# Embedding gate: bias added on VectorE, gate block by block, projection behind the third FFN group, and a norm that subtracts over both halves first

## The chip, the cores and the metric

The kernel runs on one core of one Trainium2 chip. The metric is device time in microseconds (us) from the start to the end of one execution, as a median over runs. In the text PE is TensorE (matmuls), PEld its weight loads, DVE is VectorE, ACT is ScalarE, POOL is GpSimd and SP is SyncE, which issues the DMAs.

## The reference, cut to what matters

A decoder of two layers works on x of 256 tokens by 1024 features in float32. Each layer is FFN, mixer, FFN and an embedding step, each followed by a norm. The mixer is forgetting attention in layer 0 and latent attention (MLA) in layer 1; neither is changed.

```python
def post_norm(x, delta, g, b):
    return layer_norm(ALPHA * x + delta, g, b)

for i in range(DEPTH):
    ...
    x = post_norm(x, 0.5 * swiglu(x, ffn1_w_in[i], ffn1_w_out[i]), ln_g[i, 0], ln_b[i, 0])
    ...                                     # the mixer, with its norm ln_g[i, 1]
    x = post_norm(x, 0.5 * swiglu(x, ffn2_w_in[i], ffn2_w_out[i]), ln_g[i, 2], ln_b[i, 2])
    gate = jax.nn.sigmoid(x @ ple_w_gate[i] + ple_b_gate[i])
    x = post_norm(x, gate * (p[i] @ ple_w_proj[i]), ln_g[i, 3], ln_b[i, 3])
```

`ple_w_gate` is 1024 x 1024 per layer, `ple_b_gate` one row of 1024, `p[i]` 256 x 256 and `ple_w_proj` 256 x 1024. A `layer_norm` needs mean and variance over the 1024 features of a token, then (x - mean) * rstd * g + b.

## The kernel before

**Tiles.** The 256 tokens are two tiles, t = 0 and 1, of 128 partitions; `x[t]` is 128 x 1024. `xT` holds x transposed, which matmuls use as the stationary operand (`L473` is the transpose on PE, `XT(t)` does one tile in two halves of four). Each product is formed in three matmuls (`mm3`, `L469`): every operand is split into a high part in a short-mantissa form (ACT copies, `L163` for weights, `L478` for activations) and a low part (DVE subtracts, `L164` and `L479`), and high x high, high x low and low x high are added in PSUM.

**Weights.** `Stream` loads weights in groups into three staging buffers (`raw`, DMAs on SP) in the order in which they are first used. It splits a unit into one of ten slots (`hl`), or into larger tiles that are lent to it while nobody else uses them (`ota`, `otb`, `qk`, `fs`). A slot comes free after the last use of its unit. `pump`, called after each `mm3`, emits the next split when a slot is free, its load has arrived by the planner's clock, and the planned time of ACT and DVE is at most 1.6 us ahead of PE's; `use` forces a split that is still missing. So the order of splits among other work on ACT and DVE is set as the program is written out, by planned times that `S.busy` keeps. `tl` gets a tile by its tag; a tag with one buffer (`PT`, `gb`) waits for the last reader of what it held.

**PSUM.** `bank` hands out eight banks: four `y`, two `h`, two `tr`.

**FFN** (`ffn`): 11 chunks of 256 features. `H` and `HT` compute a chunk's gate and up projections, `W` adds its part of the output. Chunks 0 and 1 come first, then groups (2, 3, 4), (5, 6, 7), (8, 9, 10), each followed by the `W` of finished chunks; `W` of chunks 8 to 10 runs for tile 0, then its norm is emitted, then for tile 1, with `XT(0)` inside. `at` lists work to do ahead of a chunk. `EDGE` gives the number of dummy transposes of the identity ahead of the first chunk of the second and third group.

**Embedding step.** `ple_load` (ahead of chunk 4 of the second FFN) loads p, `ple_transpose` (chunk 5) transposes it, `ple_project` (chunk 8) multiplies it with `ple_w_proj` in `h` banks, four results of 128 x 512, which ACT copies to `pj` (`L736`). `ple` then does the gate for tile 0 ("row 0") and tile 1 ("row 1"). It first puts the bias into the banks: the bias row is a weight unit of one partition (`pb`), and a row of ones as stationary operand spreads it over 128 partitions, in two matmuls per block (high and low part). The gate matmuls follow, for each k of 8 over both blocks of 512 columns; in layer 1, row 1 goes block by block in four quarters of 256. `post` takes the sigmoid (`L764`), multiplies by the projection (`L765`), adds to x (`L530`) and takes statistics (`L531`). `ln_apply` merges them (`L539`, `L540`), takes the power on POOL (`L541`) and applies the norm in four DVE passes over halves (`L546`): subtract mean and multiply by g, then multiply by rstd and add b. It does half 0 entirely, then half 1, except in the kernel's last norm (`last`), where both subtractions come first. `load_gb` loads g and b, spread over the partitions, once the tile `gb` is free. Behind layer 0's embedding step stands layer 1's first FFN, which begins with the key/value projection (`kv_down`).

Of the kernel before, what the change touches and what calls it, by code (L numbers as in the profile page):

```python
# [15 lines left out]
D = 1024  # L16
# [236 lines left out]

WIDTH = {"kd": 1280, "dq": 1536, "kq": 1280, "kvv": 1024, "ff": 1024, "pb": 64}

# [12 lines left out]
def unit_of(key, raw):  # L268

    k, u = key[0], key[-1] % 2  # L270
    if k in ("win", "fv"):
        return raw.rearrange("p (k c) -> p k c", c=512)[:, 2 * u : 2 * u + 2, :], 128, 1024
    if k in ("wout", "fo", "pg", "pp", "mo", "qr"):
        return raw[:, 1024 * u : 1024 * u + 1024], 128, 1024
    if k in ("fk", "fq"):
        return raw.rearrange("p (k c) -> p k c", c=256)[:, :, 128 * u : 128 * u + 128], 128, 1024
    if k == "pb":
        return raw[0:1, 0:1024], 1, 1024
# [12 lines left out]
    raise KeyError(key)  # L291


def make_loads(a):
# [3 lines left out]
    def loads(q, g, raw, fine, between):  # L298
# [25 lines left out]
        elif k in ("wout", "fo", "pg", "pp", "mo"):  # L324
# [10 lines left out]
            q.dma_start(raw.rearrange("p (k c) -> p k c", c=1024), rows(w, 2 * i, 2))  # L335
        elif k == "pb":
            q.dma_start(raw[0:1, 0:1024], a["ple_b_gate"][g[1] : g[1] + 1, :])
        elif k == "kd":
# [43 lines left out]
class Trunk:  # L382
# [33 lines left out]
    def setup(self):  # L416
# [5 lines left out]
        self.mhalf = one([128, 1], F32, "mhalf")  # L422
        self.ones = one([1, 128], F32R, "ones")
        self.xT = one([128, 2, 2, 8, 128], F32R, "xT")
# [15 lines left out]
        for c0 in (0, 256):  # L440
# [3 lines left out]
            )  # L444
        nc.gpsimd.memset(self.ones.bitcast(F32), 1.0)
        self.S.lend("ota", "otb", "qk", "fs")
# [86 lines left out]

    def ln_apply(self, t, st, eps, last=False):
        nc = self.nc
# [7 lines left out]
        hs = [slice(512 * n, 512 * n + 512) for n in range(2)]  # L543
        for i, n in ((0, 0), (0, 1), (1, 0), (1, 1)) if last else ((0, 0), (1, 0), (0, 1), (1, 1)):
            xs = self.x[t][:, hs[n]]
            nc.vector.scalar_tensor_tensor(  # L546
                xs, xs, rs if i else mv[:, 0:1], self.gb[:, i, hs[n]],
                op0=ALU.mult if i else ALU.subtract, op1=ALU.add if i else ALU.mult,
            )
# [8 lines left out]
    def ffn(self, li, which, lni, kv=False, at=None, cold=False):  # L558
# [125 lines left out]
        for group in GROUPS:  # L684
            for c in group:
                for f in at.get(c, ()):
                    f()
                if c == 4:
                    self.load_gb(li, lni)
                HT(c, (lambda: T(1)) if c == 2 else None, EDGE[li, which] if c == group[0] > 2 else 0)  # L690
            if kv and done == 0:
                self.flush()
                self.kv_transpose()
            while done < min(group[-1] + 1, n - STAG):
                W(done, both)
                done += 1
        for c in range(n - STAG, n):
            W(c, (0,))
# [24 lines left out]
    def ple_project(self, li):  # L723
# [14 lines left out]
    def ple(self, li, last):  # L738
        nc, S = self.nc, self.S
        y, st = {}, {}  # L740

        def bias(t, blocks):
            w = self.use(("pb", li))
            for c0, c1 in blocks:
                y[t, c0] = self.bank("y")
                for i in range(2):
                    self.mm(
                        y[t, c0][:, 0 : c1 - c0], self.ones, w[0:1, i, c0:c1], i == 0, False
                    )

        def gate(t, k, blocks):
            w = self.use(("pg", li, k))
            for c0, c1 in blocks:
                self.mm3(
                    y[t, c0][:, 0 : c1 - c0], lambda i: self.xT[:, t, i, k, :],
                    lambda i: w[:, i, c0:c1], False, k == 7,
                )

        def post(t, c0, c1):
            if t not in st:  # L760
                st[t] = [self.tl([128, 4, 6], F32, "st4", 2), self.tl([128, D], F32, "g4", 5), 0]
            s, sg, j = st[t]
            g = sg[:, c0:c1]
            nc.scalar.activation(g, y[t, c0][:, 0 : c1 - c0], AF.Sigmoid)  # L764
            nc.vector.tensor_tensor(g, g, self.pj[:, 2 * t + c0 // 512, c0 % 512 : c0 % 512 + c1 - c0], op=ALU.mult)  # L765
            self.ln_stats(s[:, j, :], t, c0, c1 - c0, g, ALPHA)
            self.S.busy(act=c1 - c0, dve=c1 - c0)
            st[t][2] = j + 1

        full = ((0, 512), (512, 1024))  # L770
        bias(0, full)
        for k in range(8):
            if k == 6:
                self.XT(1)
            gate(0, k, full)
        for c0, c1 in full:
            post(0, c0, c1)
        self.ln_apply(0, st[0][0][:, 0:2, :], LN_EPS)
        quarters = tuple((c, c + 256) for c in range(0, 1024, 256))
        bias(1, full if not last else quarters)  # L780
        if not last:
            for k in range(8):
                if k == 6:
                    self.XT(0)
                gate(1, k, full)
            for c0, c1 in full:
                post(1, c0, c1)
            self.ln_apply(1, st[1][0][:, 0:2, :], LN_EPS)
            S.lend("ota")
        else:  # L790
            self.store(0)
            for c0, c1 in quarters:
                for k in range(8):
                    gate(1, k, ((c0, c1),))
                post(1, c0, c1)
            self.ln_apply(1, st[1][0], LN_EPS, True)
            self.store(1)
# [289 lines left out]
    def kv_setup(self):  # L1087
        self.kvn = self.tl([128, QR], F32, "nrm", 1)[:, 0:256]
        if not self.rec:
            self.dma(self.kvn, pbcast(self.a["kv_norm"], 256))  # L1090
            for t in range(2):
                self.dma(self.rope[:, t], self.a["rope"][128 * t : 128 * t + 128])
        self.kvtok = self.tl([128, 2, 768], F32, "PT", 1)

    def rms_scale(self, src, n, junk):
# [279 lines left out]
    def run(self):  # L1375
# [4 lines left out]
            5: [self.ple_transpose],  # L1380
            8: [lambda: self.ple_project(li)],
        }
# [68 lines left out]
```

## Time and profile before

| | |
|---|---|
| median of 3 runs (lowest, highest) | 1101.17 us (1100.28, 1101.95) |
| span of the profiled execution | 1100.3 us; no other time is given for it |
| mean granted clock of TensorE | 0.997 |
| PE / PEld busy | 1080.1 us (98%) / 976.7 us (89%) |
| DVE / ACT / POOL busy | 711.5 us (65%) / 542.5 us (49%) / 79.7 us (7%) |
| HBM read | 196.81 MB, 180 GB/s over the span |

How to read the rows shown further on. A row of the timeline has the start in us from the start of the span, the time to the end of the last of the merged instructions, engine, source line, operation, output<-inputs, shapes and count; in brackets stands the engine's idle time ahead of it and what ended that. A row of the groups by line has count | busy us, mean ns | idle us ahead, and what ended it. Matmuls overlap, so a stream of them is read by the distance of their starts. Line numbers are those of the kernel above.

### The profile page before, as it was taken

To read this page: it belongs to the slowest core of one execution; us is meant where nothing else is said; L and a number is where in the kernel's file an instruction comes from. 1 tells how busy PE (TensorE), PEld (TensorE's weight loads), DVE (VectorE), ACT (ScalarE), POOL (GpSimd) and SP (SyncE) were. 2 spreads that over 40 slices of the span, in tenths; PEclk is the share of its full clock that TensorE was granted. 3 is DMA by queue.
4 is the path that set the end of the run, shared out by engine and by line. 5 is a ranking of instruction groups with operands and counts; after the bars stand their busy time and mean duration, and the time that the engine had idled before them with its cause. 6 is when DMAs were issued, how large, how long until landed. Compare 5 with 4: busy or idle time off the path is not lost. (4 is left out here: it accounts for less than half of the span.)

```text
span 1100.3 us, 17702 instructions
## 1 busy us (share of the span) xinstructions
PE 1080.1 (98%) x7186; PEld 976.7 (89%) x7186; DVE 711.5 (65%) x1006; ACT 542.5 (49%) x790; POOL 79.7 (7%) x130
## 2 busy tenths in 40 slices
PE   9999999999999999999999999998999999999997
PEld 6989998899879899997899999987899789898986
DVE  5765545788896555458975453487766885454576
ACT  5554433567645534434655353345655474445421
POOL 0000000313100000001320000011111000000000
PEclk9999999999999999999999999999999999999998
DMA  8896652553458756445677564353533678555502
GB/s 280 282 294 223 214 185 72 162 165 135 145 170 279 253 198 191 154 163 163 187 259 245 190 193 143 104 150 107 162 111 111 215 245 276 177 187 175 182 8 77
DMA packets 150676, 199.00 MB, mean 181 GB/s; under 512 B 11842, under 2 KB 128578, under 8 KB 150596
## 3 DMA queue, kind: packets, MB, share of 16 engines
q1 hardware_dynamic: 150596, 197.88, 55.6%
q8 instruction: 56, 0.92, 0.3%
q14 instruction: 24, 0.20, 0.1%
HBM read 196.81 MB, written 1.05 MB: 180 GB/s over the span
## 5 line engine op out<-in xcount | busy, mean ns | idle before, releaser
L164 DVE TENSOR_TENSOR hl<-raw,hl 128x1024 fp32r<-128x1024 f32 (+3 forms) x287 | 334.5, 1184 | 172.5 <-ACT hl L163 171.7
L163 ACT ACTIVATE hl<-raw 128x1024 fp32r<-128x1024 f32 (+3 forms) x287 | 286.9, 1021 | 198.6 <-PE y L469 82.2
L469 PE MATMUL h<-xT,hl 128*128 128x256 f32 x2016 | 239.9, 278 | 1.7 <-DVE P L613 0.7
L469 PEld LDWEIGHTS h<-xT,hl 128*128 128x128 f32 x2016 | 234.1, 188 | 3.7 <-DVE P L613 0.9
L469 PE MATMUL y<-hl,g 128*128 128x512 f32 x816 | 189.6, 390 | 0.0
L469 PEld LDWEIGHTS y<-hl,g 128*128 128x128 f32 x816 | 152.2, 188 | 31.0
L469 PE MATMUL tr<-xT,hl 128*128 128x256 f32 x864 | 102.0, 277 | 0.0
L469 PEld LDWEIGHTS tr<-xT,hl 128*128 128x128 f32 x864 | 100.0, 188 | 0.1
L469 PE MATMUL h<-hl,xT 128*128 128x512 f32 (+1 forms) x396 | 94.7, 388 | 0.4 <-DVE hl L164 0.3
L469 PEld LDWEIGHTS h<-hl,xT 128*128 128x128 f32 x396 | 72.1, 188 | 17.1 <-DVE hl L164 2.2
L541 POOL TENSOR_TENSOR rs<-ve,mhalf 128x1 f32<-128x1 f32 x16 | 15.2, 951 | 827.1 <-DVE ve L540 827.1
L469 PE MATMUL y<-hl,xT 128*128 128x512 f32 (+2 forms) x312 | 61.0, 351 | 0.0
L469 PEld LDWEIGHTS y<-hl,xT 128*128 128x128 f32 x312 | 50.8, 188 | 7.9 <-issue 0.7
L478 ACT ACTIVATE xT<-tr 128x512 fp32r<-128x512 f32 x36 | 20.2, 597 | 58.9 <-PE tr L473 58.9
L479 DVE TENSOR_TENSOR g<-P,g 128x512 fp32r<-128x512 f32 x36 | 24.9, 693 | 34.5 <-ACT g L478 34.5
L478 ACT ACTIVATE g<-P 128x512 fp32r<-128x512 f32 x36 | 22.8, 634 | 40.3 <-DVE P L648 29.4
L164 DVE TENSOR_TENSOR otb<-raw,otb 128x1024 fp32r<-128x1024 f32 (+1 forms) x20 | 24.1, 1203 | 18.9 <-ACT otb L163 18.9
L469 PE MATMUL y<-hl,ota 128*128 128x512 f32 x144 | 36.0, 393 | 0.0
L164 DVE TENSOR_TENSOR qk<-raw,qk 128x1024 fp32r<-128x1024 f32 x21 | 25.8, 1230 | 14.4 <-ACT qk L163 14.4
L469 PE MATMUL tr<-xT,qk 128*128 128x256 f32 x264 | 31.9, 277 | 0.0
L479 DVE TENSOR_TENSOR xT<-tr,xT 128x512 fp32r<-128x512 f32 x36 | 23.3, 683 | 13.3 <-ACT xT L478 13.3
L469 PEld LDWEIGHTS tr<-xT,qk 128*128 128x128 f32 x264 | 30.9, 188 | 0.0
(232 smaller groups left out, 1371.0 us busy)
## 6 DMA issues: line engine op xcount, KB each, us to landing
raw<-in_ffn_w_in_dram SPq DMA_DIRECT2D x172, 512.0 KB, 4.9
raw<-in_ffn_w_out_dram SPq DMA_DIRECT2D x44, 1024.0 KB, 5.1
raw<-in_fox_w_in_dram SPq DMA_DIRECT2D x12, 1024.0 KB, 5.3
raw<-in_ple_w_gate_dram SPq DMA_DIRECT2D x8, 1024.0 KB, 5.0
raw<-in_mla_w_o_dram SPq DMA_DIRECT2D x8, 1024.0 KB, 6.0
gb<-in_ln_g_dram SPq DMA_DIRECT2D x8, 512.0 KB, 6.3
gb<-in_ln_b_dram SPq DMA_DIRECT2D x8, 512.0 KB, 7.4
raw<-in_fox_w_o_dram SPq DMA_DIRECT2D x4, 1024.0 KB, 5.1
```

The lines of the kernel that those rows point to most:

```text
L163: nc.scalar.activation(hi[:, c], src[:, c], AF.Copy)
L164: nc.vector.tensor_tensor(lo[:, c], src[:, c], hi[:, c].bitcast(F32), op=ALU.subtract)
L469: self.nc.tensor.matmul(out, lhsT, rhs, start=start, stop=stop)
L478: self.nc.scalar.activation(hi, src, AF.Copy)
L479: self.nc.vector.tensor_tensor(lo, src, hi.bitcast(F32), op=ALU.subtract)
L541: nc.gpsimd.tensor_tensor(rs, ve, self.mhalf, op=ALU.pow)
```

## The change

The bias row is loaded by `ple_load` as one broadcast DMA of 512 KB into the tile `PT`, and DVE adds it to each block as it leaves PSUM; the sigmoid then works in place, from SBUF. The weight unit `pb`, the row of ones and the one-row matmuls are gone. `kv_setup` no longer takes `PT`; `kv_down(0)` does, after `ple`. The gate runs block by block in both rows: all eight k for one block, `post` for it, then the next block. Layer 1's row 1 has blocks of 512, 256 and 256. `XT(1)` stands ahead of k = 4 of row 0's second block; in layer 0, row 1's first `post` is put off until `XT(0)`, ahead of k = 3 of the second block. `ple_project` runs behind chunk 10, ahead of the last `W` products, in `tr` banks. `EDGE` is keyed by FFN and chunk: the second FFN has 1 dummy transpose at chunk 5 as before and 4 instead of 1 at chunk 8; the first has 4 at both, as before. `ln_apply` always does both subtractions first.

```diff
+FULL = ((0, 512), (512, 1024))
-EDGE = {(0, "ffn1"): 4, (0, "ffn2"): 1, (1, "ffn1"): 4, (1, "ffn2"): 1}
+EDGE = {("ffn1", 5): 4, ("ffn1", 8): 4, ("ffn2", 5): 1, ("ffn2", 8): 4}
...
-        for i, n in ((0, 0), (0, 1), (1, 0), (1, 1)) if last else ((0, 0), (1, 0), (0, 1), (1, 1)):
+        for i, n in ((0, 0), (0, 1), (1, 0), (1, 1)):
...
-                HT(c, (lambda: T(1)) if c == 2 else None, EDGE[li, which] if c == group[0] > 2 else 0)
+                HT(c, (lambda: T(1)) if c == 2 else None, EDGE.get((which, c), 0))
...
+        for f in at.get(n, ()):
+            f()
         for c in range(n - STAG, n):
             W(c, (0,))
...
+        self.bg_row = self.tl([128, 2, 768], F32, "PT", 1).rearrange("p a b -> p (a b)")[:, 0:D]
+        if not self.rec:
+            self.dma(self.bg_row, pbcast(self.a["ple_b_gate"][li], D))
...
-                ps = self.bank("h")
+                ps = self.bank("tr")
...
-        def bias(t, blocks):
-            w = self.use(("pb", li))
-            for c0, c1 in blocks:
-                y[t, c0] = self.bank("y")
-                for i in range(2):
-                    self.mm(
-                        y[t, c0][:, 0 : c1 - c0], self.ones, w[0:1, i, c0:c1], i == 0, False
-                    )
...
+                if k == 0:
+                    y[t, c0] = self.bank("y")
                 self.mm3(
                     y[t, c0][:, 0 : c1 - c0], lambda i: self.xT[:, t, i, k, :],
-                    lambda i: w[:, i, c0:c1], False, k == 7,
+                    lambda i: w[:, i, c0:c1], k == 0, k == 7,
                 )
-        def post(t, c0, c1):
+        def post(t, *blocks):
             if t not in st:
                 st[t] = [self.tl([128, 4, 6], F32, "st4", 2), self.tl([128, D], F32, "g4", 5), 0]
+            sg = st[t][1]
+            for c0, c1 in blocks:
+                g = sg[:, c0:c1]
+                nc.vector.tensor_tensor(g, y[t, c0][:, 0 : c1 - c0], self.bg_row[:, c0:c1], op=ALU.add)
+                nc.scalar.activation(g, g, AF.Sigmoid)
+            for c0, c1 in blocks:
+                scaled(t, c0, c1)
+
+        def scaled(t, c0, c1):
             s, sg, j = st[t]
             g = sg[:, c0:c1]
-            nc.scalar.activation(g, y[t, c0][:, 0 : c1 - c0], AF.Sigmoid)
             nc.vector.tensor_tensor(g, g, self.pj[...], op=ALU.mult)
             self.ln_stats(s[:, j, :], t, c0, c1 - c0, g, ALPHA)
...
+        def row(t, blocks, at={}):
+            for i, (c0, c1) in enumerate(blocks):
+                for k in range(8):
+                    if (i, k) in at:
+                        at[i, k]()
+                    gate(t, k, ((c0, c1),))
+                if (i, 8) not in at:
+                    post(t, (c0, c1))
+            self.ln_apply(t, st[t][0][:, 0 : len(blocks), :], LN_EPS)
+
+        row(0, FULL, {(1, 4): lambda: self.XT(1)})
         if not last:
+            def between():
+                self.XT(0)
+                post(1, FULL[0])
+            row(1, FULL, {(0, 8): None, (1, 3): between})
             S.lend("ota")
         else:
             self.store(0)
+            row(1, ((0, 512), (512, 768), (768, 1024)))
             self.store(1)
...
     def kv_down(self, t):
+        if t == 0:
+            self.kvtok = self.tl([128, 2, 768], F32, "PT", 1)
...
-            8: [lambda: self.ple_project(li)],
+            NCH: [lambda: self.ple_project(li)],
```

More of the change, by code (lines that the diff above doesn't have):

```diff
@@ L422, in setup @@
         self.mhalf = one([128, 1], F32, "mhalf")
-        self.ones = one([1, 128], F32R, "ones")
         self.xT = one([128, 2, 2, 8, 128], F32R, "xT")
@@ L532, in ln_stats, with ln_apply @@
         self.S.busy(dve=2 * w)
-    def ln_apply(self, t, st, eps, last=False):
+    def ln_apply(self, t, st, eps):
         nc = self.nc
@@ L740, in ple @@
         y, st = {}, {}
-        def bias(t, blocks):
-            w = self.use(("pb", li))
-            for c0, c1 in blocks:
-                y[t, c0] = self.bank("y")
-                for i in range(2):
-                    self.mm(
-                        y[t, c0][:, 0 : c1 - c0], self.ones, w[0:1, i, c0:c1], i == 0, False
-                    )
+        quarters = tuple((c, c + 256) for c in range(0, 1024, 256))
         def gate(t, k, blocks):
@@ L762, in post @@
+        def scaled(t, c0, c1):
             s, sg, j = st[t]
             g = sg[:, c0:c1]
[L764 removed]
             nc.vector.tensor_tensor(g, g, self.pj[:, 2 * t + c0 // 512, c0 % 512 : c0 % 512 + c1 - c0], op=ALU.mult)
             self.ln_stats(s[:, j, :], t, c0, c1 - c0, g, ALPHA)
[L767 removed]
+            self.S.busy(act=c1 - c0, dve=2 * (c1 - c0))
             st[t][2] = j + 1
[L770 removed]
@@ L771, in ple @@
[L771 to L780, printed above, removed]
-        if not last:
[L782 to L788, printed above, removed]
+        def row(t, blocks, at={}):
[7 more added lines that the diff above has]
+            self.ln_apply(t, st[t][0][:, 0 : len(blocks), :], LN_EPS)
@@ L791, in ple @@
             self.store(0)
[L792 to L796, printed above, removed]
+            row(1, ((0, 512), (512, 768), (768, 1024)))
             self.store(1)
```

8 lines of the change are left out of this document (1 added, 7 removed).

## The prediction

> **What bounds the kernel now.** I read the page first, then the time by stages, the groups by line, and last the timeline at the places that the diff touches.
>
> ```profile
> span 1100.3 us, 17702 instructions
> PE 1080.1 (98%) x7186; PEld 976.7 (89%) x7186; DVE 711.5 (65%) x1006; ACT 542.5 (49%) x790; POOL 79.7 (7%) x130
> ```
>
> TensorE (PE) is busy in 98% of the span, so a matmul taken out saves its time, as long as the next matmul's operands are there earlier too. That condition decides this case, and the stages show where it is weak.
>
> ```profile
> 502.00:513.80 11.80, 11.80 (x55) 9.30 (x54) 10.04 (x17) 3.52 (x7) 0.92 (x1) 1.00 0.73 235
> 513.80:528.00 14.20, 14.20 (x66) 11.23 (x65) 12.29 (x18) 7.75 (x10) 0.92 (x1) 1.00 0.43 137
> 536.00:550.00 14.00, 14.00 (x75) 12.16 (x75) 12.82 (x15) 9.42 (x15) 9.12 (x12) 1.00 0.67 212
> ```
>
> Columns: stretch, length, then busy time of PE, PEld, DVE, ACT, POOL. Over the whole span VectorE (DVE) is busy 65%; in the embedding step of layer 0 and the FFN behind it, it is busy 85 to 92% (10.04 of 11.80, 12.29 of 14.20, 12.82 of 14.00), and that is where the change gives it more work. PE is not idle there at all, at a granted clock of 1.00.
>
> **A. The bias matmuls go.** Three stretches in the timeline: projection of the FFN, bias, gate of row 0 in layer 0; and gate, bias, gate at row 1 of layer 1.
>
> ```profile
> 500.72 1.64 PE L469 MATMUL y<-hl,g 128*128 128x512 f32 x6
> 503.42 1.65 PE L469 MATMUL y<-hl,xT 128*128 128x512 f32 x6
> 1009.03 5.61 PE L469 MATMUL h<-hl,g 128*128 128x512 f32 x24
> 1076.62 3.01 PE L469 MATMUL y<-hl,xT 128*128 128x512 f32 x12
> 1080.74 11.57 PE L469 MATMUL y<-hl,xT 128*128 128x256 f32 x96
> L469 PE MATMUL y<-hl,ones 1*128 1x256 f32 (+1 forms) x12 | 2.5, 336 | 0.0
> L469 PE MATMUL y<-fs,ones 1*128 1x512 f32 x8 | 2.4, 419 | 0.0
> ```
>
> The row of 24 gives the pitch of 512-column matmuls: (5.61 - 0.39) / 23 = 0.227 us, where 0.39 is one matmul's length; the row of 96 gives (11.57 - 0.28) / 95 = 0.119 for 256 columns. Six at 0.227 from 500.72 end at 502.08 and the gate starts at 503.42: four one-row matmuls hold PE for 1.34, not for 4 x 0.227 = 0.91, so changing to and from the one-row form costs about 0.4 more. Row 1 of layer 1: 1076.62 + 12 x 0.227 = 1079.34, gate at 1080.74, 1.40. The 20 bias matmuls stand in four such groups: 3 x 1.34 + 1.40 = 5.4 us off PE. Bounds: 4.5 (pitch alone) and 5.4. Layer 1's first two quarters become one block: 24 x 0.227 = 5.45 for 48 x 0.119 = 5.71, 0.2 less. Sum -5.6. The splitting of the bias row (one ACT and one DVE pass per layer) and its turn in the three staging buffers go as well, off the path.
>
> **B. The projection moves; one edge grows.** Before, it stood ahead of chunk 8 and its evacuation held that chunk's bank.
>
> ```profile
> 1014.50 0.95 PE L469 MATMUL h<-xT,hl 128*128 128x256 f32 x6
> 1015.65 5.21 PE L469 MATMUL h<-xT,hl 128*128 128x256 f32 x42 [0.20 <-ACT ota L736]
> 1048.96 4.29 PE L469 MATMUL y<-hl,g 128*128 128x512 f32 x18
> 1050.49 1.05 ACT L163 ACTIVATE hl<-raw 128x1024 fp32r<-128x1024 f32 x1
> L736 ACT ACTIVATE ota<-h 128x512 f32<-128x512 f32 x8 | 4.8, 595 | 3.5 <-PE h L469 3.5
> 1075.83 1.04 PE L473 MATMUL tr<-ident,x 128*128 128x128 f32 x8
> ```
>
> Six matmuls from 1014.50 at 0.119 end at 1015.21; the next starts at 1015.65: 0.44 lost per layer, -0.9 for two. Chunk 8 gets three more dummy transposes: (1.04 - 0.27) / 7 = 0.11 each, 6 x 0.11 = +0.65, since I see no wait there for them to fill. The projection itself costs the same 24 matmuls, but now the third of its four results needs the bank of the first back, 12 x 0.227 = 2.72 after its start. Where it will start, the projection of chunk 8 starts today (1048.96), and ACT splits a weight until 1050.49 + 1.05 = 1051.54; behind that in ACT's queue the evacuation takes 0.60, to 1052.14, and the bank is wanted at 1051.68: 0.5 of waiting, twice, +1.0 (0 if the split comes later, 1.5 if two come first). Its weights' load and two splits move with it behind three chunks on SP, ACT and DVE; they are wanted 35 us later as well. B is +0.75, between -0.25 and +1.25.
>
> **C. Every norm subtracts over both halves first.** The last norm of the kernel has that order already, so both orders stand in the timeline.
>
> ```profile
> 1059.77 0.74 DVE L546 SCALAR_TENSOR_TENSOR x<-x,mv,gb 128x512 f32<-128x512 f32 x1
> 1060.95 0.75 DVE L546 SCALAR_TENSOR_TENSOR x<-x,rs,gb 128x512 f32<-128x512 f32 x1 [0.44 <-POOL rs L541]
> 1062.41 0.75 DVE L546 SCALAR_TENSOR_TENSOR x<-x,rs,gb 128x512 f32<-128x512 f32 x1
> 1094.51 1.40 DVE L546 SCALAR_TENSOR_TENSOR x<-x,mv,gb 128x512 f32<-128x512 f32 x2
> 1095.84 1.41 DVE L546 SCALAR_TENSOR_TENSOR x<-x,rs,gb 128x512 f32<-128x512 f32 x2
> 309.87 0.63 PE L473 MATMUL tr<-ident,x 128*128 128x128 f32 x4 [0.82 <-DVE x L546]
> 728.08 0.63 PE L473 MATMUL tr<-ident,x 128*128 128x128 f32 x4 [0.66 <-DVE x L546]
> 870.08 0.75 DVE L546 SCALAR_TENSOR_TENSOR x<-x,rs,gb 128x512 f32<-128x512 f32 x1 [1.15 <-DMA gb<-in_ln_b_dram]
> 875.22 1.19 PE L469 MATMUL h<-qk,xT 128*128 128x512 f32 x4 [0.29 <-DVE xT L479]
> 899.72 2.33 PE L469 MATMUL h<-xT,hl 128*128 128x256 f32 x18 [0.69 <-DVE P L613]
> ```
>
> Old order: 1059.77 to 1063.16, 3.39. New: 1094.51 to 1097.25, 2.74. So 15 norms get 0.65 shorter, and their first half is ready 0.14 later (2.07 against 1.93 after the start). That pays only where PE waits for a norm. At 309.87 and 728.08 it waits for the second half: 0.65 at the first; at the second I take 0.2 (estimate), because the next V product waits behind the norm in DVE's queue for work that POOL holds anyway. At 870.08 the norm waits for its late bias row; with both subtractions first, that wait is filled, and PE's waits of 0.29 and 0.69 behind it should go, 1.0 together. C is -1.9, between 0 (another late operand takes each wait's place) and -2.5.
>
> **D, E. VectorE's new work.** The nearest rows for an add out of a bank are the FFN's products, for the sigmoid the old one.
>
> ```profile
> L648 DVE TENSOR_TENSOR P<-P,h 128x512 f32<-128x512 f32 x20 | 13.8, 688 | 20.8 <-PE h L469 12.7 <-ACT P L647 8.1
> L613 DVE TENSOR_TENSOR P<-P,h 128x256 f32<-128x256 f32 x16 | 6.6, 415 | 4.7 <-ACT P L612 4.7
> L764 ACT ACTIVATE g<-y 128x512 f32<-128x512 f32 x6 | 3.5, 600 | 0.4
> L164 DVE TENSOR_TENSOR hl<-raw,hl 128x1024 fp32r<-128x1024 f32 x255 | 308.7, 1229 | 165.5 <-ACT hl L163 165.1
> 509.68 0.75 DVE L546 SCALAR_TENSOR_TENSOR x<-x,rs,gb 128x512 f32<-128x512 f32 x1
> 522.74 0.75 DVE L546 SCALAR_TENSOR_TENSOR x<-x,rs,gb 128x512 f32<-128x512 f32 x1
> 525.00 1.03 PE L473 MATMUL tr<-ident,x 128*128 128x128 f32 x8
> 503.42 0.73 ACT L163 ACTIVATE hl<-raw 128x640 fp32r<-128x640 f32 x1
> 511.08 0.82 DVE L164 TENSOR_TENSOR hl<-raw,hl 128x640 fp32r<-128x640 f32 x1
> 1086.79 0.75 DVE L546 SCALAR_TENSOR_TENSOR x<-x,rs,gb 128x512 f32<-128x512 f32 x1
> 1092.35 0.38 ACT L764 ACTIVATE g<-y 128x256 f32<-128x256 f32 x1 [2.44 <-PE y L469]
> ```
>
> A block of 512 now takes DVE 0.69 (add), about 0.7 idle for the sigmoid (0.60 and two hand-overs), and three passes of 0.69: 3.5; a block of 256 takes 0.42 + 0.5 + 1.3 = 2.2. Behind a waiting add stand the splits of coming weights and the low part of the next transposed rows.
>
> Layer 0 (D), on the old clock with the bias out: row 0 starts at 502.1, row 1 at 502.1 + 48 x 0.227 + 0.87 (eight transposes) = 513.8. DVE's norm of the FFN's second tile, 510.4 before, ends at about 510.0; block 0 then runs to 513.5, the low parts of row 1's input (two passes, 1.3) to 514.8, one queued split to 516.0. Row 1's third matmul wants the first low part at 514.3 and has it at 514.2: just in time. Block 1 to 519.5, statistics 0.4, norm 2.74: first half ready at 522.0. The transposes of tile 0 stand 33 matmuls into row 1, 521.3 (before there was room: norm done 523.49, transposes 525.00). So +0.8. The gate's weights are now kept until row 1's second block, 5.4 us longer, so three splits that DVE could do early go behind that norm. With DVE at 88%, PE 2.7 us ahead of its old time must give some of it back in the first FFN chunks: I take 1.1. D is +1.9, between 0 and 2.7, where layer 0's whole saving is lost.
>
> Layer 1 (E): row 1 ends 3 us earlier, but its three blocks come after the norm of tile 0. That starts from row 0's end, 1079.34 today less its own bias group of 1.34, 1078.0, and 0.1 more until DVE has it; it takes 3.5 + 0.4 + 2.74: 1084.7 (before 1087.54). Then 3.5 + 2.2 + 2.2: 1092.6. From the last sigmoid's end (1092.73) to the norm's end (1097.25) is 4.5 today, 1.3 of it three passes over 256; the rest, 3.2, follows as it is: 1095.8, 1.45 earlier than 1097.25. Of the 2.95 that A gives layer 1 (1.34 + 1.40 + 0.2), 1.5 is lost. E is +1.5, between 0.5 and 2.9.
>
> The broadcast of the bias row is 512 KB more on SP ahead of the norm's rows at chunk 4, some 1.6 us at the 343 GB/s of this stretch:
>
> ```profile
> 355.00:365.00 10.00, 10.00 (x91) 10.00 (x90) 6.42 (x7) 6.10 (x7) 0.00 (x0) 1.00 1.01 343
> ```
>
> I cost it at nothing: chunk 4's weights are split by then, and chunk 5 is 30 us off; with that cover gone it is 1.6 per layer. The wait of the key/value copy for the bias row's last reader is nothing: that add is done a norm earlier.
>
> **Sum.** -5.6 + 0.75 - 1.9 + 1.9 + 1.5 = -3.35. The profiled execution has no other time beside its span of 1100.3, which is 0.9 below the runs' median of 1101.17; so 1097.0 for the span and 1097.8 for the median.
>
> D and E rest on DVE taking its work in order. The rows above show it once: the split whose high part ACT ended at 504.15 got its low part at 511.08, behind the whole norm that ended at 510.43. [...]
>
> **Rivals.** (1) All hidden: DVE catches up in layer 0, the bank's wait in B does not come: D 0, B -0.25: -6.25, span 1094.05, median 1094.9. For it: DVE has 3 us free in those 28; against: its new work comes in waits, not only in busy time. (2) DVE is the clock of the whole step: D 2.7, E 2.9, C 0.4 of its 1.9: -5.6 + 0.75 - 0.4 + 5.6 = +0.35, no change: 1101.5. The norms then do not do what they say. For it: 12.82 of 14.00; against: PE never waits there today. (3) Slower: the kept slots. Row 1's first block frees no slot, and if the FFN's first four splits, 4 x 1.23 = 4.9, all land behind its last norm and on PE's path, D is 2.7 + 4.9; with E 2.9 and C as forecast: -5.6 + 0.75 - 1.9 + 7.6 + 2.9 = +3.75, 1104.9. It decides from 4 us on PE's path beyond D's 2.7; against it: a first-sweep order that asks for high parts first.
>
> **Chances.** 0.2% is 2.2 us, about what a measurement of this kernel can tell. Forecast (-2.2 to -5) 0.45, its own range 1096.2 to 1099.0; rival 1 0.2; rival 2 0.25; rival 3 0.1. So faster 0.65, same 0.25, slower 0.1. Range: rival 1 with C at its bound of -2.5, 1094.3, to rival 2, 1101.5.
>
> **What would show it.** A: no one-row matmuls, PE's gate directly behind the projection. B: a wait of the projection on ACT ota of about 0.5. C: norms of 2.74, no PE wait near 309 and 899. D: PE waiting on DVE x or xT near 520 and on hl near 540. E: DVE, not PE, ending the last chain, the last add starting over 1 us after its matmuls. The prediction is wrong if PE waits more than 3 us between 500 and 550, or if the chain ends on PE.

## The result, and the profile after

Median 1095.34 us after (1094.80 to 1095.58, 4 runs) against 1101.01 us before (4 runs): ratio 0.9947, 95% interval 0.9935 to 0.9959, 5.7 us faster. Measured a second time, the same pair gave 1094.40 against 1101.69 (`r_after`, below), ratio 0.9934 (0.9921 to 0.9946). The forecast was 1097.8, range 1094.3 to 1101.5: the time lies in the range, but below the forecast's own band of 1096.2 to 1099.0, and the gain is 2.3 us larger than the sum. Two executions of each kernel were profiled (the second ones are the runs `r_before` and `r_after`), and the second of before is what explains the difference. From the page of after:

```profile
span 1093.6 us, 17616 instructions
PE 1072.9 (98%) x7148; PEld 970.6 (89%) x7148; DVE 712.1 (65%) x1010; ACT 539.3 (49%) x787; POOL 81.3 (7%) x129
## 4 chain that ended last, share of the span: by engine, by line
DVE 1%; ACT 0%; issue 0%; DVEq 0%
```

The same line of the chain in before:

```profile
PE 17%; DVE 2%; DMA 1%; ACT 1%; issue 1%; SPq 0%; POOL 0%; DVEq 0%; ACTq 0%
```

PE lost 7.2 us of busy time between these two profiles, and 5.2 between the second ones (1077.4 to 1072.2). The chain that ended last is new in kind: as far back as it is traced (16 us) it holds no PE at all. The end of layer 1 belongs to DVE and ACT now.

To see where the time went, I cut the span at events that both kernels have, and compare the lengths of the pieces (worked out from the timelines; the times named are those of the first profile of before, and a chunk counts from the start of its silu):

| stretch | before, 1st | before, 2nd | after, 1st | after, 2nd |
|---|---|---|---|---|
| start to chunk 2 of the first FFN, 0 to 43.2 | 43.20 | 43.79 | 43.62 | 42.89 |
| to the transposes at 308.4 | 265.22 | 265.15 | 265.36 | 265.07 |
| norm there, to the transposes at 320.0 | 11.54 | 11.54 | 10.76 | 10.70 |
| to chunk 7 of the second FFN, 428.2 | 108.26 | 108.24 | 108.24 | 108.30 |
| chunks 8 to 10, projection, to the transposes at 499.9 | 71.70 | 70.43 | 70.78 | 70.82 |
| embedding step of layer 0, to chunk 2 at 570.0 | 70.05 | 70.13 | 68.07 | 68.07 |
| to the transposes at 726.8 | 156.85 | 156.85 | 156.84 | 156.84 |
| latent attention and its norms, to 910.0 | 183.21 | 182.50 | 182.00 | 181.53 |
| to chunk 7, 992.3 | 82.24 | 82.25 | 82.24 | 82.24 |
| chunks 8 to 10, projection, to 1064.0 | 71.70 | 70.43 | 70.78 | 70.79 |
| embedding step of layer 1, to PE's last matmul | 28.34 | 28.34 | 25.23 | 25.23 |
| to DVE's last pass | 4.93 | 4.93 | 6.57 | 6.58 |
| to the end of the span | 3.08 | 3.07 | 3.07 | 3.08 |
| span | 1100.32 | 1097.65 | 1093.56 | 1092.15 |

Most pieces repeat to 0.1 us; the start and the latent attention vary more. Three things stand out. The embedding step shrinks as forecast. The end on DVE grows as forecast. And chunks 8 to 10 take 71.70 us in one execution of the kernel before and 70.43 in the other, in both layers: the same program, 1.27 us apart each time. The prediction was made on the longer of the two.

**Two paces.** Rows of 96 matmuls of 256 columns: in the first profile of before (one of chunks 5 to 7, then one of 8 to 10), in the second, and in after:

```profile
406.89 11.04 PE L469 MATMUL h<-xT,hl 128*128 128x256 f32 x96
473.61 11.47 PE L469 MATMUL h<-xT,hl 128*128 128x256 f32 x96
```
```profile
473.29 11.04 PE L469 MATMUL h<-xT,hl 128*128 128x256 f32 x96
```
```profile
1026.88 11.04 PE L464 MATMUL h<-xT,hl 128*128 128x256 f32 x96
```

With 0.28 as one matmul's length the pitch, the time from start to start, is (11.47 - 0.28) / 95 = 0.1178 us in the row at 473.61 and 0.1133 in the others. In the first profile of before the granted clock is 1.00 in both its rows, from 406.89 to 417.90 us and from 473.61 to 484.90. Once it has settled, a stream here keeps its pace ("rhythm" in the expectations) to its last matmul (each row of 24 from 459 to 473 us takes 2.99 us in the first profile of before and 2.88 in the second): 288 x 0.0045 = 1.3 us for chunks 8 to 10, each layer.

### The profile page after: what moved, and what is told of

Its sections match the earlier page's. It is cut to its first block, busy times and chain, and to the rows that moved or that the text cites. A ratio compares the mean times of both kernels' runs of the same rounds, so it can differ in the third digit from the quotient of the medians.

```text
span 1093.6 us, 17616 instructions
## 1 busy us (share of the span) xinstructions
PE 1072.9 (98%) x7148; PEld 970.6 (89%) x7148; DVE 712.1 (65%) x1010; ACT 539.3 (49%) x787; POOL 81.3 (7%) x129
## 5 line engine op out<-in xcount | busy, mean ns | idle before, releaser
L464 PE MATMUL h<-xT,hl 128*128 128x256 f32 x2064 | 243.7, 278 | 1.0 <-DVE qk L474 0.6
L464 PEld LDWEIGHTS h<-xT,hl 128*128 128x128 f32 x2064 | 238.3, 188 | 2.4 <-DVE qk L474 0.8
L464 PE MATMUL y<-hl,g 128*128 128x512 f32 x804 | 186.6, 390 | 0.0
L464 PE MATMUL tr<-xT,hl 128*128 128x256 f32 x840 | 98.9, 277 | 0.0
L464 PEld LDWEIGHTS tr<-xT,hl 128*128 128x128 f32 x840 | 96.9, 188 | 0.1
L464 PE MATMUL y<-hl,xT 128*128 128x512 f32 (+2 forms) x276 | 57.8, 363 | 0.0
L464 PEld LDWEIGHTS y<-hl,xT 128*128 128x128 f32 x276 | 47.5, 188 | 7.4
L164 ACT ACTIVATE qk<-raw 128x1024 fp32r<-128x1024 f32 x21 | 22.2, 1058 | 19.3 <-PE tr L464 6.6
L464 PE MATMUL tr<-xT,otb 128*128 128x256 f32 x264 | 31.7, 276 | 0.0
L464 PEld LDWEIGHTS tr<-xT,otb 128*128 128x128 f32 x264 | 30.7, 188 | 0.0
```

Of the source, the lines that this page charges most:

```text
L164: nc.scalar.activation(hi[:, c], src[:, c], AF.Copy)
L464: self.nc.tensor.matmul(out, lhsT, rhs, start=start, stop=stop)
```

## The experiments

They ran on three chips; a ratio is to the kernel before on the same chip. Its medians there were 1099.29 (e1 to e4), 1101.69 (`r_before`, `r_after`, e7, e8) and 1099.03 us (e5, e6, e9, e10). The changed kernel itself ran beside e7 and e8 only, so what e2, e4, e6, e9 and e10 change against it is read from stretches of the trace.

**e2, one dummy transpose in the changed kernel.**

```diff
-EDGE = {..., ("ffn2", 5): 1, ("ffn2", 8): 4}
+EDGE = {..., ("ffn2", 5): 1, ("ffn2", 8): 1}
```

> The changed kernel with one dummy transpose instead of four ahead of chunk 8 of the second FFN; the projection stays behind chunk 10. Theory (rhythm set by the transposes): chunks 8 to 10 fall back to 118 ns, +1.3 us a layer, less 0.33 for the three transposes: +1.0 a layer, +2.0 us in all, ratio to the changed kernel 1.0018, to the kernel before 0.9965. Rival (the wait on ACT ota or the projection ahead of the chunk sets the rhythm): they stay at 113.7, and three transposes less give -0.33 a layer, -0.65 in all, ratio to the kernel before 0.994.

Median 1096.44, ratio 0.9974 (0.9964 to 0.9984). Its timeline:

```profile
443.74 0.27 PE L468 MATMUL h<-ident 128*128 128x128 f32 x1
443.77 11.55 PE L464 MATMUL h<-xT,hl 128*128 128x256 f32 x96
472.12 5.82 PE L464 MATMUL h<-xT,hl 128*128 128x256 f32 x48
```

(5.82 - 0.28) / 47 = 0.1179: the slower pace, in both layers, and chunks 8 to 10 with the projection take 71.72 us, 0.94 more than in the changed kernel, as the theory said (+1.0). So moving the projection does not by itself bring the quicker pace, and the slower one does not need the wait on ACT `ota` ahead of the chunk: there is none here.

**e1, four dummy transposes in the kernel before.**

```diff
-EDGE = {(0, "ffn1"): 4, (0, "ffn2"): 1, (1, "ffn1"): 4, (1, "ffn2"): 1}
+EDGE = {("ffn1", 5): 4, ("ffn1", 8): 4, ("ffn2", 5): 1, ("ffn2", 8): 4}
...
```

> The kernel before, with four dummy transposes instead of one ahead of chunk 8 of each layer's second FFN; the projection stays where it was, directly ahead of them. Theory (rhythm): the number of transposes ahead of a run of 256-column matmuls settles at which of two rhythms, 113.3 or 118 ns from start to start, it goes through. Then chunks 8 to 10 go from 118.1 to 113.7 ns a matmul, 288 x 4.6 ns = 1.3 us a layer; 3 more transposes at 0.11 take 0.33 of it, or fill part of the 0.44 wait on ACT ota. Net -1.0 to -1.3 a layer, -2.0 to -2.6 us in all, ratio 0.998. Rival (wait): the slow rhythm comes from the projection's wait on ACT ota ahead of the chunk, so the chunks stay at 118 and the time goes up by 0 to 0.65 us. Rival (no rhythm): the change's 2.6 us beyond the forecast of part B lie elsewhere; no change of the distance from chunk 8 to chunk 10.

The stretch of chunks 8 to 10 is 70.43 us in both layers, 1.27 less than in the first profile of before. The three dummies fill most of the wait on ACT `ota` (3 x 0.11 of 0.44, an estimate from the rows of before), so this run alone doesn't tell the theory from the rival; the next one does. Where they fill a wait they cost nothing: the second profile of before, with one, has the same 70.43. But the median is 1100.35, ratio 1.0012 (1.0002 to 1.0022), not the 0.998 expected. The kernel before took 1099.29 on that chip, near the 1099.43 of the execution that was profiled in the quicker pace, so there may have been nothing left to gain; no execution of it was profiled there. In e1's trace the piece of latent attention and norms takes 184.1 us, 1.6 more than in the second profile of before, and the chunks nothing; that piece varies from profile to profile, as e3 shows.

**`r_before` and `r_after`, both kernels once more.**

> The kernel before once more, for the rhythm of chunks 8 to 10 behind one dummy transpose. If one transpose leaves the rhythm open (e3 went through them at 113.7 ns with one, the kernel before and e2 at 118), it can come out either way here, and the span shows it: about 1100.3 us at 118, 1097.7 at 113.7. If the rhythm is fixed by the program, 118 again and a span of 1100.

The pace is 113 ns this time, span 1097.65, and the wait ahead of chunk 8 is there all the same:

```profile
452.09 7.76 PE L469 MATMUL h<-xT,hl 128*128 128x256 f32 x66 [0.19 <-ACT ota L736]
```

The same row of the first profile, at 451.60, takes 8.04. So the wait does not bring the slower pace, and e2 has that pace without the wait: the rival of e1 and e2 is out. The profiled run (1099.43) is one of the lowest of the kernel's runs on that chip; the other ten of `r_before` took 1101.4 to 1103.0.

> The changed kernel once more, beside the others of this call. With four transposes ahead of every group the rhythm is 113.7 ns in all six late chunks of both second FFNs: median 1093.5 to 1095.5 us, ratio to the kernel before 0.995 to 0.997 (less than the first 0.9947 if the kernel before is in the fast rhythm on this chip).

1094.40, ratio 0.9934. Runs of the changed kernel lie within 0.4 us here, those of the kernel before within 4.3.

Over all 14 profiles, eight groups of chunks each: behind four or five transposes (102 groups) the pace settles at 113 ns in every one; behind a single one (chunk 8, ten groups in five executions) it is 118 in both layers of before, e2 and e8, and 113 in both layers of `r_before` and e3. So one transpose leaves the pace open, and four settled it. What decides it stays open. It is not a property of the execution as a whole: the first 24 matmuls of chunk 2, behind four transposes of data, settle at 118 ns in some FFNs and at 113 in others of one execution (in after 118 at 32.5 us and 113 at 334.7), so the number of transposes is not all of it either.

**e5, part B alone.** The kernel before with the projection behind chunk 10 in `tr` banks, and four dummies at chunk 8.

```diff
-            8: [lambda: self.ple_project(li)],
+            NCH: [lambda: self.ple_project(li)],
```

> The kernel before with part B alone: projection behind chunk 10 on the other pair of banks, four dummy transposes ahead of chunk 8. Theory (rhythm is left open by one transpose and settled by four): chunks 8 to 10 at 113.7 ns in both layers in this and every execution; to an execution of the kernel before in the fast rhythm the part costs what the record said, +0.75 us (its two waits for a bank and six more transposes, less the stall ahead of chunk 8), to one in the slow rhythm it gains 1.9. So a profiled span of about 1098.4 (fast execution of before 1097.65 + 0.75), the ratio of medians 0.998 to 1.0007, by how many executions of before fall in the slow rhythm. Rival (part B is a gain by itself, whatever the rhythm): span under 1096.

Median 1100.81, ratio 1.0013 (1.0004 to 1.0022), 1.8 us longer and above the 0.998 to 1.0007 expected: alone, part B gains nothing. The stretch takes 70.79 us in both layers, 0.72 more in sum than in the execution of before with the quicker pace, 1.8 less than in the one with the slower. In the profiled run another 1.2 over `r_before` lies again in the stretch of latent attention. The medians of e1 and e5 are near their profiled runs, so this is no single outlier; whether the edits bring it about or the chip does is not shown.

**e3 and e4, the norms' order.** e3 is the kernel before with only the new order, e4 the changed kernel with the old one.

```diff
-        for i, n in ... if last else ((0, 0), (1, 0), (0, 1), (1, 1)):
+        for i, n in ((0, 0), (0, 1), (1, 0), (1, 1)):
```

> The kernel before, with only the norms' new order (both halves subtracted first, then both scaled): part C alone. By the traces of before and after: -0.78 at the transposes of layer 0 near 309 us, about -0.35 net near 728, -0.86 near 875 to 900; in sum -2.0 us, ratio 0.998, if the parts add up; on the record of the prediction -1.9. At the end of layer 1 the norms of 2.74 instead of 3.39 also let the second row's products start sooner, but there TensorE bounds the kernel before, so nothing more. Rival: the gain at 309, 728 and 900 came from the rows' new timing and not from the order; then 0 to -0.8.

Ratio 0.9984 (0.9975 to 0.9992), -1.8 us. Against the second profile of before, 0.79 of it is at the transposes of 309 us and 0.96 in the latent attention. At 309, the second profile of before and the first of after:

```profile
310.39 0.63 PE L473 MATMUL tr<-ident,x 128*128 128x128 f32 x4 [0.82 <-DVE x L546]
```
```profile
308.98 1.29 PE L468 MATMUL tr<-ident,x 128*128 128x128 f32 x8
```

All eight transposes now run as one group; the wait for the second half is gone. The latent attention begins with the same case. The second profile of before, and the first of after:

```profile
727.39 0.63 PE L473 MATMUL tr<-ident,x 128*128 128x128 f32 x4 [0.67 <-DVE x L546]
```
```profile
723.66 1.23 PE L468 MATMUL tr<-ident,x 128*128 128x128 f32 x8
```

From these transposes to the next group on another tile (744.86 in the first profile of before) PE takes 18.03 to 18.08 us in the six profiles with the old order and 17.39 to 17.42 in the eight with the new: 0.65, in every execution. The rest of the stretch depends on two broadcast rows, g and b of a norm near 870 us, which in some executions arrive late. In e5 (old order) the norm waits for both, in after for one:

```profile
868.26 0.75 DVE L546 SCALAR_TENSOR_TENSOR x<-x,mv,gb 128x512 f32<-128x512 f32 x1 [0.74 <-DMA gb<-in_ln_g_dram]
869.67 0.75 DVE L546 SCALAR_TENSOR_TENSOR x<-x,rs,gb 128x512 f32<-128x512 f32 x1 [0.66 <-DMA gb<-in_ln_b_dram]
```
```profile
865.12 1.42 DVE L541 SCALAR_TENSOR_TENSOR x<-x,mv,gb 128x512 f32<-128x512 f32 x2 [0.36 <-DMA gb<-in_ln_g_dram]
```

How late they are changes from profile to profile, and in `r_before` neither is waited for. The whole stretch took 182.5 to 184.1 us in the six profiles with the old order and 181.5 to 182.4 in the eight with the new (e2 is the 182.4).

> The changed kernel with the old order of the norms' passes (all but the last norm). If part C is worth 2.0 us by itself, +2.0 us and, since VectorE now bounds the last row, 0.65 more for each of the two norms that stand in its chain near the end (FFN tile 1, gate tile 0): +3.3 us at the most; 0.65 more in layer 0 if VectorE is late there too (transposes near 520 us). So +2.0 to +4 us, ratio to the changed kernel 1.002 to 1.0035. Rival (order only matters where TensorE waits, and those waits are covered otherwise in the changed kernel): under +1 us.

1100.37, ratio 1.0009 (1.0001 to 1.0018): without the new order the whole change is worth nothing on that chip. Against the two profiles of after its span, less the differing start, is 5.5 and 6.2 us longer, outside my +2 to +4. 2.9 of that is layer 0's embedding step:

```profile
521.92 0.63 PE L468 MATMUL tr<-ident,x 128*128 128x128 f32 x4 [0.17 <-DVE x L541]
523.37 0.63 PE L468 MATMUL tr<-ident,x 128*128 128x128 f32 x4 [0.82 <-DVE x L541]
542.65 0.73 PE L464 MATMUL h<-hl,xT 128*128 128x512 f32 x2 [0.70 <-DVE hl L165]
543.91 3.37 PE L464 MATMUL h<-hl,xT 128*128 128x512 f32 x20 [0.53 <-DVE hl L165]
```

DVE's chain there starts 0.4 later, behind the norm of the FFN's tile 0; three more norms stand in it, each 0.65 longer, and the splits behind them take 0.5 more: 2.9. PE waits for that chain at tile 0's transposes and in the next FFN. In the changed kernel only one such wait is left (below).

**e8, part A alone.** e4 with the projection ahead of chunk 8 and one dummy there: the kernel before with nothing but the bias on DVE, block by block.

> The kernel before with part A alone: the bias on VectorE, block by block; the projection ahead of chunk 8, one dummy transpose there, and the old order of the norms. By the record of the prediction, parts add up: A -5.6, D +1.9, E +1.5, so -2.2 us to the kernel before. By the ledger of the two traces (A -5.8, D +0.7, E +1.65): -3.45. By what e4 showed (the old order costs the changed kernel 5.3 us of span, where it gave the kernel before 2.0 alone), the part alone comes out 3.3 worse than the ledger: -0.1 us, and up to +1.5 if the rhythm of the kernel before is the fast one and this one's is not.

1101.88, ratio 1.0002 (0.9993 to 1.0011): the part that takes PE's 5.8 us away is worth nothing by itself, as the last of the three expectations said and the forecast's own sum (-2.2) did not. By stretches against the first profile of before, which has the same pace: layer 0's embedding step is 0.97 us longer, though PE's work shrank by 2.7 (D is 3.7), and layer 1's is 0.80 shorter where PE's shrank by 3.1 (E is 2.3).

**e6, no add.** The gate's sigmoid reads the bank.

```diff
-                nc.vector.tensor_tensor(g, y[t, c0][:, 0 : c1 - c0], self.bg_row[:, c0:c1], op=ALU.add)
-                nc.scalar.activation(g, g, AF.Sigmoid)
+                nc.scalar.activation(g, y[t, c0][:, 0 : c1 - c0], AF.Sigmoid)
```

> The changed kernel without VectorE's add: the gate's sigmoid reads the bank directly, so the bias is left out of the computation and the one-row matmuls stay out too. What is left to gain is what the change lost to VectorE. By the record, D 1.9 and E 1.5: -3.4 us to the changed kernel. By the ledger of the traces, D 0.7 and E 1.65: -2.3, bounded at the end by TensorE (its end + sigmoid 0.42 + 3 x 0.44 + 0.4 + 2.74). So -2.0 to -2.4, span about 1090.

1092.24, ratio 0.9939 (0.9926 to 0.9951); span 1090.2. Layer 0's embedding step takes 67.37 us, 0.70 less than after's 68.07, and the end behind PE's last matmul 4.90, 1.67 less than in after: D and E of the table of parts below ("the ledger" of the expectations), measured by taking their cause away. At the end the multiplies wait for a sigmoid that itself waits for PE:

```profile
1079.94 0.42 DVE L766 TENSOR_TENSOR g<-g,ota 128x256 f32<-128x256 f32 x1 [0.36 <-ACT g L759]
1082.66 0.42 DVE L766 TENSOR_TENSOR g<-g,ota 128x256 f32<-128x256 f32 x1 [1.38 <-ACT g L759]
```

**e7, the waits for the sigmoid filled at the end.** In the last row, each block's add and sigmoid are issued ahead of the previous block's sum.

```diff
...
+            self.ln_apply(0, ..., lambda: added(1, *last3[0]))     # called ahead of the last pass
...
+            scaled(1, *last3[0], lambda: added(1, *last3[1]))      # called behind the multiply
+            scaled(1, *last3[1], lambda: added(1, *last3[2]))
+            scaled(1, *last3[2])
```

> The changed kernel with another order at the end of layer 1: each block's add and sigmoid are issued ahead of the previous block's weighted sum and statistics (the first block's ahead of the last pass of tile 0's norm), so that VectorE has work in the 0.70, 0.48 and 0.48 us in which it waits for a sigmoid. Theory (VectorE is the bound of the end): these 1.66 us go, until TensorE's end at 1083.9 bounds it: last block add to norm 1083.95 + 0.41 + 0.48 + 3 x 0.44 + 0.4 + 2.74 = 1089.3 against 1090.5. So -0.9 to -1.2 us to the changed kernel, ratio to it 0.999. Rival (TensorE or the stores set the end): 0.

1093.63 against `r_after`'s 1094.40 on the same chip, span 1.0 less. The end of DVE in after, then in e7 (where `L767` is the add and `L773` the multiply):

```profile
1079.55 0.69 DVE L759 TENSOR_TENSOR g<-y,PT 128x512 f32<-128x512 f32 x1
1080.93 0.69 DVE L767 TENSOR_TENSOR g<-g,ota 128x512 f32<-128x512 f32 x1 [0.70 <-ACT g L760]
1083.00 0.41 DVE L759 TENSOR_TENSOR g<-y,PT 128x256 f32<-128x256 f32 x1
1083.89 0.43 DVE L767 TENSOR_TENSOR g<-g,ota 128x256 f32<-128x256 f32 x1 [0.48 <-ACT g L760]
1086.04 0.42 DVE L767 TENSOR_TENSOR g<-g,ota 128x256 f32<-128x256 f32 x1 [0.48 <-ACT g L760]
```
```profile
1078.86 0.69 DVE L773 TENSOR_TENSOR g<-g,ota 128x512 f32<-128x512 f32 x1
1079.82 0.42 DVE L767 TENSOR_TENSOR g<-y,PT 128x256 f32<-128x256 f32 x1 [0.27 <-PE y L464]
1082.53 0.42 DVE L767 TENSOR_TENSOR g<-y,PT 128x256 f32<-128x256 f32 x1 [0.64 <-PE y L464]
1083.67 0.41 DVE L773 TENSOR_TENSOR g<-g,ota 128x256 f32<-128x256 f32 x1
```

The three waits for ACT (1.66) are gone, and two for PE (0.91) stand in their place: DVE ends 5.61 behind PE instead of 6.58, and the chain that ended last runs over PE again (20% of the span).

**e9, the projection over both pairs of banks**, on top of e7.

```diff
-                ps = self.bank("tr")
+                ps = self.bank("h" if n else "tr")
```

> e7 (end of layer 1 with interleaved blocks), and the projection's four results taken in turn from both pairs of banks, so that its third no longer waits for ACT to empty the first. Theory: the wait of 0.37 in the projection goes in both layers, -0.74 us to e7; at the end of layer 1, where VectorE and TensorE both start from the FFN's end, the whole of it comes through. Span about 1090.4. Rival: the wait moves to the next user of the other pair, the low parts of the transposed rows or the first gate's bank: 0.

1092.77, ratio 0.9942 (0.9929 to 0.9954) to a kernel before at 1099.03; span 1090.6, 0.55 less than e7's on another chip. The stretch of chunks 8 to 10 is 70.27 in both layers, 0.52 less per layer than in e7; the other stretches of the two profiles differ by 0.5 the other way, 0.27 of it ahead of chunk 7. In after, and in e9:

```profile
477.83 2.90 PE L464 MATMUL tr<-hl,g 128*128 128x512 f32 x12
480.93 3.02 PE L464 MATMUL tr<-hl,g 128*128 128x512 f32 x12 [0.21 <-ACT ota L736]
483.79 5.60 PE L464 MATMUL y<-hl,g 128*128 128x512 f32 x24
```
```profile
477.12 1.54 PE L464 MATMUL tr<-hl,g 128*128 128x512 f32 x6
482.57 3.79 PE L464 MATMUL y<-hl,g 128*128 128x512 f32 x16
```

Start to start the projection took 5.96 in after and takes 5.45 = 24 x 0.227 now: both its waits, 0.38 ahead of the third result and 0.13 ahead of the fourth, are gone. I had read only the first. (Its last row counts the matmuls up to 486 us.) This is the best version run that computes the gate in full.

**e10, the same filling in layer 0.**

```diff
             def between():
+                added(1, *FULL[0])
                 self.XT(0)
-                post(1, FULL[0])
...
+            scaled(1, *FULL[0], lambda: added(1, *FULL[1]))
```

> e9, and the interleaved order in layer 0 too: row 1's first add ahead of the transposes of tile 0, its second add between the first block's multiply and sum. It fills two of VectorE's four waits of 0.70 there, 1.4 us; TensorE's waits for it in the next FFN's first chunks are 0.46 + 0.33. Theory (D is VectorE's lateness there): -0.6 to -0.8 us to e9. Rival (what is late there are the weights' splits behind the norm, in an order that the planner sets): 0 or a small loss, since the transposes of tile 0 get their low parts 0.7 later.

The theory missed. 1093.33, ratio 0.9946 (0.9933 to 0.9958); the embedding step takes 68.02 us, in e9 68.05. PE's wait of 0.31 at 539 us is gone, and another has come. ACT and DVE in e9 at the high and low parts of tile 0's transposed rows, then the same in e10, with PE behind it:

```profile
520.03 1.06 ACT L473 ACTIVATE xT<-tr 128x512 fp32r<-128x512 f32 x2
521.75 1.28 DVE L474 TENSOR_TENSOR xT<-tr,xT 128x512 fp32r<-128x512 f32 x2
```
```profile
521.98 0.68 DVE L767 TENSOR_TENSOR g<-y,PT 128x512 f32<-128x512 f32 x1
522.70 0.63 ACT L768 ACTIVATE g<-g 128x512 f32<-128x512 f32 x1 [2.35 <-DVE g L767]
523.24 1.07 ACT L473 ACTIVATE xT<-tr 128x512 fp32r<-128x512 f32 x2
523.85 1.29 DVE L474 TENSOR_TENSOR xT<-tr,xT 128x512 fp32r<-128x512 f32 x2 [1.19 <-ACT xT L473]
524.60 2.62 PE L464 MATMUL h<-hl,xT 128*128 128x320 f32 x16 [0.16 <-DVE xT L474]
```

The low parts come 1.9 later (2.10, less 0.23 by which e10 starts behind), not the 0.7 expected: the sigmoid stands ahead of the high parts in ACT's queue and waits there for DVE's add (ACT is idle for 2.35 us, though the transposes ended at 520.57), so DVE then waits 1.19 for ACT. ACT took its work in order here, the sigmoid at 522.70 and only then the high parts at 523.24; I had counted on that for DVE alone. PE then waits 0.16 for the first low part, the second tile's transposes stand 0.55 later from the start of the stretch, and the gain is used up.

## Why the prediction was right, and where it was not

Against the second profile of before, which has the pace of after, the table gives each part by itself:

| part | predicted | measured | how |
|---|---|---|---|
| A, bias off PE | -5.6 | -5.8 | row 0 of layer 0 -1.35; its row 1 taken as the same; layer 1 -3.11 |
| B, projection and edge | +0.75 | +0.75 | +0.39 and +0.36; with e5, +0.72 |
| C, norms | -1.9 | -1.8 | 309 us -0.84; 728 us -0.66; the late rows and behind -0.32 |
| D, DVE in layer 0 | +1.9 | +0.6 | 68.07 - 70.13 + 2 x 1.35 = 0.64; e6 0.70 |
| E, DVE at the end | +1.5 | +1.65 | 6.58 - 4.93; e6 1.67 |
| sum | -3.35 | -4.6 | span -5.5, of which -0.9 is the start |

**A was right**, in each group that was read, and what it said of the conditions was too: matmuls taken out pay only if the next operands come earlier. e8 shows the condition unmet: A alone, 0.

**B was right as a sum, and missed the pace.** The bank's wait was put at 0.5 and is 0.51 (0.38 + 0.13), the stall of 0.44 went, and three dummies cost what is left, 0.36 - 0.51 + 0.44 = 0.29, for 0.33. What failed is the base of the forecast: it took the profiled execution of before as the one time of that kernel. That execution ran chunks 8 to 10 at 118 ns; with four dummies instead of one the pace was 113 in every profile, worth 1.27 per layer against an execution like that and nothing against one like the second. The prediction's price of a dummy, 0.11 with nothing to gain, missed what they settle. The clue was in the trace: the row of 96 at 473.61 takes 11.47 where chunks of the other groups have 11.04. So -4.6, and up to 2.5 us more where the execution of before falls in the slower pace; the medians (-5.7, -7.3) may hold a mixture, which the runs without a profile can't show.

The base was off in a second way. The forecast set its median 0.9 us above its span (1101.17 and 1100.3). In every later run of the kernel before that has both on record, the time is 1.7 to 1.9 us above the span of the same run; in the four timed runs of after it is 2.0. By that, the profiled execution would have taken about 1102.1 us (an estimate), longer than each of the four timed ones. Span against span, 1097.0 was forecast and 1093.6 came.

**C was right in its sum, by luck.** At 309 us 0.65 was forecast and 0.8 came. At 728 us, 0.2 was forecast, because the next product would wait all the same, and the whole 0.65 came, in every execution. For the late rows, 1.0 was forecast from one execution in which the b row came 1.15 late; `r_before` waits for no row, and against it 0.3 is left. PE's wait near 899, forecast to go, is 0.38 in the first profile of after and absent in the second. Two errors of half a microsecond and more cancel. C was also priced only where PE waits for a norm in the kernel before. Its larger worth is in the changed kernel, where DVE is the bound in layer 0's step: 71.01 - 68.07 = 2.9 us there, and 7.24 - 6.58 = 0.66 at the end (e8 against after). D and E counted with norms of 2.74, so the sum holds; a reader of the table who drops C alone would be 3.6 us off.

**D was mis-sized**, 1.9 for 0.6 to 0.7. Rows of after:

```profile
507.08 1.41 DVE L541 SCALAR_TENSOR_TENSOR x<-x,rs,gb 128x512 f32<-128x512 f32 x2
519.38 1.41 DVE L541 SCALAR_TENSOR_TENSOR x<-x,rs,gb 128x512 f32<-128x512 f32 x2
520.45 1.11 PE L468 MATMUL tr<-ident,x 128*128 128x128 f32 x8
540.27 3.36 PE L464 MATMUL h<-hl,xT 128*128 128x512 f32 x20 [0.30 <-DVE hl L165]
```

On the prediction's old clock (add 1.18, by which after is ahead at 499.93) the FFN's norm ends at 509.67, not 510.0; the first half of tile 0 is ready at 520.1 + 1.18 = 521.3, not 522.0; the transposes come at 521.6. The 0.8 there is therefore 0: a chain of eight steps summed 0.7 too long, at a place decided by 0.3. The 1.1 for the next FFN is what is left, 0.6 to 0.7. Nearly all of it is at a wait on a weight's low part at 540, the kind that the prediction named: the ten matmuls from 537.43 take 2.84 to the next start, for 10 x 0.227 = 2.27.

**E was right**: the last chain holds DVE and ACT only, the last row's waits for the sigmoid are 0.70 and 0.48 as forecast, and DVE ends 1.65 later behind PE.

Of the rivals, the first (all hidden) comes nearest in time by another road: the bank's wait, D and E are there, and the pace made up for them. The second (DVE is the clock) describes e4 and e8, which have the old order of the norms: both are no gain. The third, kept slots, has no sign in the trace; PE waits 0.30 where it had 4.9.

## What to carry to other kernels

A matmul taken off a saturated TensorE pays only as far as the engine that now gets its work has slack in that very stage: here 5.8 us of matmuls were worth 0 by themselves, and 3.5 (5.8 less D and E) once the same change shortened VectorE's chain by the norms' order, which brought 1.8 of its own. Test the parts of a change in both directions, alone and left out, because these two numbers differ. And before a sum is set against one profiled execution, compare like stretches within it: where one group of the same shape is 4% slower than its twins, the kernel may have more than one time. A term that comes out right is no proof of its parts: C's three were 0.65, 0.2 and 1.0 by forecast and 0.8, 0.65 and 0.3 by trace.

## What the runs showed of the hardware that I had not expected

Matmuls of 256 columns went at 113.3 or 117.8 ns from start to start at the same granted clock (1.00 for both in the first profile of before), and kept their pace through 288 of them. Behind one transpose either came out, in executions of one program (before and `r_before`); where four or five stood ahead of a group of chunks it was always 113.3 (102 of 102 groups). Dummy transposes that filled a wait cost nothing (e1: 70.43 with four, `r_before` 70.43 with one), and three that filled none cost 0.29 us (by the sum under B). The arrival of a broadcast row near 870 us moves from profile to profile: the norm there waits 1.15 us for b in the first profile of before, 0.36 for g in the first of after and for neither in `r_before`; with the old order of the norm the stretch around it took 182.5 (`r_before`) to 184.1 us (e1).
